# A two-layer MLP block with seven-product matrix multiplication: five row pairs instead of six first on each range of columns, and the first pair's second range computed plainly

## The chip, the cores and the metric

The kernel runs on one core of a Trainium2 chip. The metric is the device time of one execution in microseconds (us). The kernel before took 1532.34 us, the median of three runs (1531.55 to 1533.23).

The core's engines are named as the profile names them: PE is TensorE, which multiplies matrices; DVE is VectorE; ACT is ScalarE; POOL is GpSimd; SP is SyncE, whose queue issues most of the transfers (DMA).

## The reference

```python
def reference(x, w1, w2):          # x: 8 x 1024 x 1024, w1: 1024 x 4096, w2: 4096 x 1024, float32
    h = x @ w1
    h = 0.5 * h * (1 + np.tanh(np.sqrt(2 / np.pi) * (h + 0.044715 * h ** 3)))
    return (h @ w2).astype(np.float32)
```

With the batch flattened, x has 8192 rows. The first product, the gelu and the second product follow each other.

## The kernel before

**Tiling.** The 8192 rows of x are 32 *pairs* of two blocks of 128 rows (`k` is the pair, `c` the block). The 4096 columns of w1 are two halves of 2048, and each half is cut into four *ranges* of 512 (`r`, 0 to 3). A *unit* is one pair on one range: the pair's two blocks times the range's columns in both halves of w1. Both operands are cast to float16, scaled by their largest absolute value: x for each row, w1 for each range. The factors that undo this (`us`, `rs`, `up`, `rt`) go into the gelu and into the cast of its result.

**Two kinds of units.** A *plain* unit (`Plain`) has four *quarters*, one for each row block and half of w1, each of eight matmuls of 512 columns: 32 in all. It needs only the four cast blocks of w1 (B11, B21, B12, B22). All other units (`Quad1`) use Winograd's form of Strassen's method with seven products, `m1` to `m7`, of four matmuls each: 28. They also need four sums of the blocks of w1 (`sum_w1`: T1 = B12 - B11, T3 = B22 - B12, T2 = B22 - T1, T4 = B21 - T2) and four sums of the parts of x (`sum_x`), all made by VectorE. The products add up in PSUM: ScalarE copies intermediate results out (L558, L568, L577), VectorE adds others to them (L165), ScalarE applies the gelu (L483), GpSimd scales and casts the result to g (L174), and SP stores g to DRAM (L504).

**The order of units** (L669 to L677). The first pairs, `FIRST = 6` of them, run through range 0 one after another, then through range 1, 2 and 3. After that each middle pair runs through all four ranges, and the last four pairs run range by range again. Units 0 to 5 are pairs 0 to 5 on range 0, all plain; units 6 to 11 are range 1, 12 to 17 range 2, 18 to 23 range 3. The second multiplication follows when all units are done; its work on w2 is prepared during the middle units.

**An order written out by hand.** Every engine runs its instructions in the order in which they are written. `unit(u)` (L796) issues for TensorE: m1 of unit u, m7 of unit u-1, m3 of unit u-2, m2, m6 and m5 of unit u, m4 of unit u-1. Between them are seven *slots*, and `background(u, slot)` issues what `plan(u, slot, ...)` put there: preparing work for later units. So

```python
        if u < NQ:
            q.m2()
        background(u, 3)
        if u < NQ:
            q.m6()
```

means that what is planned for slot 3 of unit u stands on each engine behind the work of m2 and ahead of that of m6. Product m6 reads T2, m5 T1, m7 T3 and m4 T4. The start, up to unit 5, runs by quarters: `p` counts them, 0 to 23 (L908), the gelu of a quarter is issued right behind it, and `early(p, ...)` plans work behind quarter p. The last quarters are those of pairs 4 and 5, one pair after the other.

**Preparing a range.** For each range r from 1 on: eight pieces of w1 are loaded from GpSimd's queue (`load_w1`, L286); the largest absolute value of each is found (`look_w1`, on VectorE L151 or on ScalarE L302); VectorE takes their maximum (`widest_w1`, L312); `scale_w1` sends it through TensorE to spread it over the partitions (L158, tile `rows`) and takes the reciprocal; the pieces are cast to blocks (`cast_w1`: VectorE L176, ScalarE L172, GpSimd L174); and VectorE makes the sums T1 to T4. Range 1 is planned at L711 to L722, ranges 2 and 3 at L723 to L742 by `u = (r - 1) * FIRST - 1`. For range 2 the sums are planned in slots 4 and 6 of unit 10 and slots 1 and 3 of unit 11, for range 3 in units 16 and 17, in this order: T1, T3, T2, T4. Range 0 is made from three scales of its own for the plain units; later GpSimd brings its blocks to one scale (`even_w1`) and its sums are made (L744 to L748).

**Preparing a pair.** Blocks of the first pairs are loaded, their largest values found on ScalarE (`look_x`, L187), cast (`cast_x`) and transposed on TensorE (`turn_x_pe`, L213) in eight matmuls with a copy by ScalarE or VectorE. Pairs 4 and 5 are planned at L692 to L703. Middle pairs are transposed by DMA from SP (`turn_x`, L204) some units ahead of their first unit `a` (L750 to L762).

Of the kernel before, what the change touches and what calls it, by code (L numbers as in the profile page):

```python
# [31 lines left out]
B11, T4, B21, B22, T1, T2, T3 = range(7)  # L32
# [48 lines left out]
def kernel(  # L81
# [19 lines left out]
    NP = T // (2 * P)  # L101
    NR = I // 2 // N
    JR = N // P
    FIRST = 6
    LAST = 4
    OPEN = 4
    WARM = 52
# [569 lines left out]
    NQ = len(order)  # L677
# [11 lines left out]
    def early(p, f, *args):  # L689
        plan(p // 4, p % 4, f, *args)  # L690

    for k in range(OPEN, FIRST):  # L692
        for h in range(2):
            c = 2 * k + h
            p = (9, 12)[k - OPEN] + h
            early(p - 1, look_x, c)
            early(p, scale_x, c)
            early(p, cast_x, c, V)
            if h:
                early(p, factors_of_block, k, 0, V)  # L700
                early(p, factors_of_block, k, 1, G)
            early((2, 5)[k - OPEN], load_x, c, wpool, "w")
            early(4 * k - 2 + 2 * h - (k > 2), turn_x_pe, c, V if h else S)  # L703
    for k in first:
        for i in range(4):
            if k < 2:
                early((16, 21)[k] + i // 2, sum_x, k, (i,))
            else:
                plan(FIRST + k - 1, 2 + i, sum_x, k, (i,))

    for n in range(8):  # L711
        early((3, 4, 5, 6, 7, 8, 9, 10)[n], load_w1, 1, n)
        early((7, 8, 10, 12, 12, 13, 14, 15)[n], look_w1, 1, n, S if n in (3, 5, 7) else V)
    early(16, widest_w1, 1)
    early(17, scale_w1, 1)
    early(17, factors, 0, FIRST, 1)
    for i, n in enumerate((4, 5, 0, 1, 6, 7, 2, 3)):
        early((17, 17, 18, 18, 19, 19, 20, 21)[i], cast_w1, 1, n, S if i % 2 and n != 3 or n == 2 else V)
    early(20, sum_w1, 1, T1)
    early(22, sum_w1, 1, T2)  # L720
    plan(FIRST, 1, sum_w1, 1, T3)
    plan(FIRST, 5, sum_w1, 1, T4)  # L722
    for r in range(2, NR):  # L723
        u = (r - 1) * FIRST - 1
        for n in range(8):
            v = u - 1 + n // 2
            if r == 2:
                plan(*((4, 1), (4, 3), (5, 0), (5, 2))[n // 2], load_w1, r, n)
                look = ((5, 3), (6, 1), (6, 1), (6, 4), (6, 3), (7, 1), (7, 1), (7, 4))[n]
                plan(*look, look_w1, r, n, S if n % 2 else V)  # L730
            else:
                plan(v, 1, load_w1, r, n)
                look = (v + 2, 1) if n == 1 else (v + 1, 3 + n % 2)
                plan(*look, look_w1, r, n, S if n == 1 else V)
        plan(u + 3, 1 if r == 2 else 5, widest_w1, r)
        plan(*((u + 3, 6) if r == 2 else (u + 4, 2)), scale_w1, r)
        plan(u + 4, 2, factors, 0, FIRST, r)
        for n in range(8):
            v, slot = ((4, 3), (4, 4), (4, 5), (5, 1), (4, 3), (4, 5), (5, 3), (4, 6))[n]
            plan(u + v, slot, cast_w1, r, n, (G, S, G, S, G, V, S, V)[n])  # L740
        for i, t in enumerate((T1, T3, T2, T4)):
            plan(u + 5 + i // 2, (4, 6, 1, 3)[i], sum_w1, r, t)  # L742
# [98 lines left out]
    with tc.manual_schedule(  # L841
        engines={
            mybir.EngineType.PE, mybir.EngineType.Activation, mybir.EngineType.DVE,
            mybir.EngineType.Pool, mybir.EngineType.SP,
        }
    ):
        load_x(0, wpool, "w")
        for n in range(2):
            load_w1(0, n)
        load_x(1, wpool, "w")  # L850
        for n in range(2, 4):
            load_w1(0, n)
        V.memset(ratio, 0.0)
        V.memset(w1c, TINY)
        S.activation(out=ratio, in_=ratio, func=ACT.Gelu_apprx_tanh)
        make_identity(nc, identity)
        V.tensor_copy(out=identity16, in_=identity)
        for c in range(2, 2 * OPEN):
            load_x(c, wpool, "w")
        for n in range(4, 8):  # L860
            load_w1(0, n)
        warm_up(identity16, WARM)
        look_x(0)
        scale_x(0)
        cast_x(0, S)
        t = x16[0]
        look_w1(0, 0)
        look_w1(0, 1, V, 0)
        look_w1(0, 1, S, 1)
        turn_x_pe(0, S)  # L870
        warm_up(t, 3)
        widest_w1(0, 2)
        look_x(1)
        scale_w1(NR + 2)
        warm_up(t, 8)
        cast_w1(0, 0, V)
        cast_w1(0, 1, V)
        plain = {k: Plain(k, 0) for k in range(FIRST)}
        pa, pc = bank("pa"), bank("pc")
        plain[0].eighth(0, 0, pa)  # L880
        look_w1(0, 2, S)
        scale_x(1)
        cast_x(1, V)
        look_w1(0, 3, V, 0)
        look_w1(0, 3, S, 1)
        widest_w1(0, 3)
        look_x(2)
        warm_up(t, 3)
        turn_x_pe(1, V)
        scale_w1(NR + 3)  # L890
        plain[0].eighth(1, 0, pc)
        cast_w1(0, 2, V)
        cast_w1(0, 3, S)
        ups_of_block(0, G)
        scale_x(2)
        cast_x(2, V)
        look_x(3)
        join_halves()
        inverse_w1(slice(NR, NR + 1), G)
        plain[0].eighth(0, 1, pa)  # L900
        turn_x_pe(2, S)
        times(rs[:, 0, :, 0], xi[:, 0:2], w1j[:, NR:NR + 1], G)
        plain[0].eighth(1, 1, pc)
        scale_x(3)
        cast_x(3, V)
        look_x(4)
        look_x(5)
        quarters = [(k, 0, half, s) for s in range(2) for k in range(OPEN) for half in range(2)]  # L908
        quarters += [(k, 0, half, s) for k in range(OPEN, FIRST) for half in range(2) for s in range(2)]
        gelus = {  # L910
            0: lambda: plain[0].gelu(0, 0, plain[0].e(), pa),
            1: lambda: plain[0].gelu(1, 0, plain[0].e(), pc),
        }

        def between(p):
            if p == 2:
                scale_x(4)
                turn_x_pe(3, V)
                cast_x(4, V)
                scale_x(5)  # L920
                cast_x(5, G)
                gelus.pop(0)()
                factors_of_block(1, 0, G)
                look_x(6)
            elif p == 3:
                turn_x_pe(4, V)
                scale_x(6)
                look_w1(0, 4)
                gelus.pop(1)()
                factors_of_block(2, 0, G)  # L930
                look_x(7)
            elif p == 4:
                turn_x_pe(5, V)
                cast_x(6, V)
                scale_x(7)
                cast_x(7, G)
                look_w1(0, 5, S)
                gelus.pop(2)()
            elif p == 5:
                turn_x_pe(6, V)  # L940
                factors_of_block(3, 0, G)
                look_w1(0, 6)
                look_w1(0, 7, S)
                widest_w1(0, 1)
                gelus.pop(3)()
            elif p == 6:
                turn_x_pe(7, V)
                scale_w1(NR + 1)
                for n in range(4, 8):
                    cast_w1(0, n, S if n % 2 else V)  # L950
                inverse_w1(slice(NR + 1, NR + 2), G)
                for k in range(OPEN):
                    factors_of_block(k, 1, G)
                gelus.pop(4)()

        for p, (k, r, half, s) in enumerate(quarters):
            if p > 1:
                gelus[p] = plain[k].quarter(half, s, ("pa", "pc")[p % 2], lambda: between(p))
            if p > 6:
                for i in list(gelus)[:2]:  # L960
                    gelus.pop(i)()
            for j in (p % 4,) if p % 4 < 3 else (3, 4, 5, 6):
                background(p // 4, j)
            let_go(len(held) - 1 if len(held) > 1 and p % 2 else 0)
        now = {}
        for u in range(FIRST, NQ):
            unit(u, None)
        V.tensor_scalar(
            out=vo, in0=xm, scalar1=w2n, scalar2=SPAN, op0=ALU.mult, op1=ALU.mult
        )  # L970
        V.tensor_scalar(out=vn, in0=vo, scalar1=-1.0, scalar2=None, op0=ALU.mult)
        for u in range(NQ, NQ + 2):
            unit(u, lambda: second(3))
        let_go()
        for u in range(NQ + 2, NQ + 6):
            for slot in range(7):
                background(u, slot)
        assert not todo, todo.keys()
        second(NP * len(PRODUCTS) - done[0])
# [28 lines left out]
```

## Time and profile before

| what | value |
|---|---|
| median of three runs | 1532.34 us (1531.55 to 1533.23) |
| the profiled execution's own time | 1531.54 us |
| its span in the profile | 1529.8 us |
| TensorE busy | 1521.2 us, 99% of the span |
| VectorE busy | 1182.0 us, 77% |
| ScalarE busy | 740.3 us, 48% |
| GpSimd busy | 476.8 us, 31% |
| granted TensorE clock | 1.00 |
| units 0 to 5 end, unit 6 begins | 62.03 us |
| mean of a sum on VectorE that makes a T, 62 to 172 us (L168, 128x2048) | 1.34 us |
| mean of an add from PSUM on VectorE (L165, 128x512) | 0.68 us |
| mean of a cast of g on GpSimd, 62 to 172 us (L174, 128x512) | 0.85 us |

The profile is of one execution. A line of a time line gives the start in us, the duration in us, the engine, the line of the kernel, the operation, what it writes and reads, its shapes, how many instructions were merged, and in brackets how long the engine had been idle before it and what ended that wait. Durations overlap a little at the ends: the next instruction of an engine starts before the last one has drained, so the step from start to start is what an instruction holds its engine. On TensorE four matmuls are listed with 1.03 us, and the next product starts 0.86 us after them.

### The profile page before, as it was taken

To read this page: it belongs to the slowest core of one execution; us is meant where nothing else is said; L and a number is where in the kernel's file an instruction comes from. 1 tells how busy PE (TensorE), PEld (TensorE's weight loads), DVE (VectorE), ACT (ScalarE), POOL (GpSimd) and SP (SyncE) were. 2 spreads that over 40 slices of the span, in tenths; PEclk is the share of its full clock that TensorE was granted. 3 is DMA by queue.
4 is the path that set the end of the run, shared out by engine and by line. 5 is a ranking of instruction groups with operands and counts; after the bars stand their busy time and mean duration, and the time that the engine had idled before them with its cause. 6 is when DMAs were issued, how large, how long until landed. Compare 5 with 4: busy or idle time off the path is not lost.

```text
span 1529.8 us, 28770 instructions
## 1 busy us (share of the span) xinstructions
PE 1521.2 (99%) x10449; PEld 1018.1 (67%) x10449; DVE 1182.0 (77%) x2410; ACT 740.3 (48%) x1322; POOL 476.8 (31%) x598
## 2 busy tenths in 40 slices
PE   9999999999999999999999999999999999999999
PEld 5444444444444444444458888888888888888888
DVE  6987788777876777574348888888888888888886
ACT  8878777777777777787662111111111111111111
POOL 4689554555666656554440000000000000000000
PEclk9999999999999999999999999999999999999999
DMA  9664989877678787875995767767766866866873
GB/s 353 235 198 137 297 263 297 252 238 244 209 238 267 225 260 227 252 200 131 280 281 135 145 135 136 149 132 134 155 137 123 158 136 124 163 128 136 151 141 81
DMA packets 460992, 293.94 MB, mean 192 GB/s; under 512 B 334001, under 2 KB 429233, under 8 KB 460849
## 3 DMA queue, kind: packets, MB, share of 16 engines
q1 hardware_dynamic: 457392, 279.52, 72.2%
q0 software_dynamic: 3456, 12.58, 2.4%
q8 instruction: 81, 1.33, 0.4%
q14 instruction: 63, 0.51, 0.1%
HBM read 96.99 MB, written 114.29 MB: 138 GB/s over the span
## 4 chain that ended last, share of the span: by engine, by line
PE 97%; DVE 1%; ACT 1%; DMA 1%; SPq 0%; issue 0%; DVEq 0%; ACTq 0%
PE pa L438 52%; PE pc L438 31%; PE pb L438 14%; DMA xn<-in_x_dram 1%; ACT junk L187 0%; DVE x L176 0%; ACT e L483 0%; DVE w1c L151 0%; PE turned L213 0%; DVE up L242 0%; SPq L286 0%; ACT w L172 0%; DVE xT L220 0%; ACT xT L218 0%; SPq L183 0%
## 5 line engine op out<-in xcount | busy, mean ns | idle before, releaser
L438 PEld LDWEIGHTS <-gs 128*128 128x128 f16 x4608 | 450.8, 98 | 53.0 <-DVE gs L168 0.2
L174 POOL TENSOR_SCALAR g<-e,rs 128x512 f16<-128x512 f32 x446 | 362.8, 823 | 283.1 <-ACT e L483 258.4
L438 PEld LDWEIGHTS <-xs 128*128 128x128 f16 x1952 | 191.0, 98 | 229.7
L165 DVE TENSOR_TENSOR e<-pc,e 128x512 f32<-128x512 f32 x244 | 162.9, 686 | 202.1 <-ACT e L577 200.8
L438 PEld LDWEIGHTS <-xT 128*128 128x128 f16 x1672 | 162.8, 98 | 193.7 <-DVE xT L220 1.6
L438 PE MATMUL pa<-w,gs 128*128 128x256 f16 x2304 | 288.3, 273 | 0.0
L438 PE MATMUL pa<-w,xT 128*128 128x512 f16 (+1 forms) x1080 | 254.7, 377 | 0.5 <-ACT xT L218 0.2
L483 ACT ACTIVATE e<-e,us 128x512 f32<-128x512 f32 x366 | 251.4, 720 | 1.8 <-DVE e L165 1.8
L438 PE MATMUL pa<-w,xs 128*128 128x512 f16 x976 | 250.5, 379 | 0.0
L438 PE MATMUL pc<-w,xs 128*128 128x512 f16 x976 | 250.5, 379 | 0.0
L438 PEld LDWEIGHTS <-gT 128*128 128x128 f16 x2048 | 200.4, 98 | 23.2
L630 ACT ACTIVATE o<-pa,vo 128x256 f32<-128x256 f32 x96 | 45.3, 472 | 332.3 <-PE pa L438 332.3
L438 PE MATMUL pc<-w,gs 128*128 128x256 f16 x1536 | 193.8, 273 | 0.0
L438 PE MATMUL pa<-w,gT 128*128 128x256 f16 x1024 | 132.7, 273 | 0.0
L438 PE MATMUL pb<-w,xT 128*128 128x512 f16 x488 | 125.2, 379 | 0.0
L626 DVE SCALAR_TENSOR_TENSOR o<-pc,vo,o 128x256 f32<-128x256 f32 x160 | 77.1, 482 | 57.8 <-PE pc L438 57.8
L568 ACT COPY e<-pa 128x512 f32<-128x512 f32 x122 | 71.6, 586 | 91.3 <-PE pa L438 87.0
L168 DVE TENSOR_TENSOR gs<-gT,gs 128x1024 f16<-128x1024 f16 x160 | 109.9, 687 | 1.2 <-DMA gT<-gd 1.2
L626 DVE SCALAR_TENSOR_TENSOR o<-pa,vo,o 128x256 f32<-128x256 f32 x192 | 92.1, 481 | 19.3 <-PE pa L438 19.1
L438 PE MATMUL pb<-w,gs 128*128 128x256 f16 x768 | 99.5, 273 | 0.0
L438 PE MATMUL pc<-w,gT 128*128 128x256 f16 x768 | 99.5, 273 | 0.0
L558 ACT COPY e<-pa 128x512 f32<-128x512 f32 x122 | 70.6, 579 | 49.9 <-PE pa L438 48.2
(106 smaller groups left out, 1451.0 us busy)
## 6 DMA issues: line engine op xcount, KB each, us to landing
gd<-g SPq DMA_DIRECT2D x504, 128.0 KB, 3.3
wn<-in_w_dram SPq DMA_DIRECT2D x72, 512.0 KB, 5.2
xn<-in_x_dram SPq DMA_DIRECT2D x64, 512.0 KB, 5.5
out_dram<-o SPq DMA_DIRECT2D x62, 512.0 KB, 4.0
w<-wd SPq DMA_DIRECT2D x25, 512.0 KB, 5.8
wn<-in_w_dram POOLq DMA_DIRECT2D x24, 512.0 KB, 5.9
wd<-wt SPq DMA_DIRECT2D x24, 512.0 KB, 4.6
gT<-gd SPq DMA_TRANSPOSE x128, 6.5
```

The costliest lines, as they stand in the source:

```text
L165: V.tensor_tensor(out=o, in0=a, in1=b, op=ALU.add)
L168: V.tensor_tensor(out=o, in0=a, in1=b, op=ALU.subtract)
L174: G.tensor_scalar(out=o, in0=i, scalar1=s, scalar2=1.0, op0=ALU.mult, op1=ALU.mult)
L438: nc.tensor.matmul(bank, lhsT=left(i), rhs=right[i], start=start and i == 0, stop=i == n - 1, skip_group_check=True,)
L483: S.activation(out=e[:, c], in_=src[:, c], func=ACT.Gelu_apprx_tanh, scale=scale)
L558: S.copy(self.e11, self.pa)
L568: S.copy(self.e12, self.pa)
L626: V.scalar_tensor_tensor(out=o, in0=ps, scalar=v, in1=o, op0=ALU.mult, op1=ALU.add)
L630: S.activation(out=o, in_=ps, func=ACT.Copy, scale=v)
```

## The change

Five pairs instead of six go first through each range (`FIRST = 5`), and the first pair is plain on range 1 too, so that there are still six plain units: pairs 0 to 4 on range 0, and pair 0 on range 1. Its quarters are the last four, p = 20 to 23, and follow pair 4. Ranges 1, 2 and 3 now begin at units 5, 10 and 15, and the middle pairs at unit 20 instead of 24. Pair 5 becomes a middle pair.

With this, plans move. For pair 4 the factors of the first block of columns go to GpSimd. The sums of x of pair 0 are no longer planned at quarter 16 but in slots 2 to 5 of unit 9; those of pairs 2, 3 and 4 go one unit ahead, to units 6, 7 and 8. The looks at range 1 stand behind quarters 9 to 16, its maximum behind quarter 16, its casts behind quarters 17 to 20 in the order of the pieces, alternating VectorE and ScalarE. The maximum and the scale of range 2 are in slots 1 and 3 of unit 8 (before: slots 1 and 6 of unit 8). By `u = (r - 1) * FIRST - 1` the casts and sums of range 2 move one unit ahead (the sums to units 9 and 10) and those of range 3 two units (to units 14 and 15), and all later plans follow the first middle unit.

```diff
-    FIRST = 6
+    FIRST = 5
...
     for k in range(OPEN, FIRST):
         for h in range(2):
             c = 2 * k + h
-            p = (9, 12)[k - OPEN] + h
+            p = 9 + h
...
             if h:
-                early(p, factors_of_block, k, 0, V)
+                early(p, factors_of_block, k, 0, G)
                 early(p, factors_of_block, k, 1, G)
-            early((2, 5)[k - OPEN], load_x, c, wpool, "w")
+            early(2, load_x, c, wpool, "w")
...
     for k in first:
         for i in range(4):
-            if k < 2:
-                early((16, 21)[k] + i // 2, sum_x, k, (i,))
+            if k == 1:
+                early(21 + i // 2, sum_x, k, (i,))
             else:
-                plan(FIRST + k - 1, 2 + i, sum_x, k, (i,))
+                plan(FIRST - 1 + (k or FIRST), 2 + i, sum_x, k, (i,))
 
     for n in range(8):
-        early((3, 4, 5, 6, 7, 8, 9, 10)[n], load_w1, 1, n)
-        early((7, 8, 10, 12, 12, 13, 14, 15)[n], look_w1, 1, n, S if n in (3, 5, 7) else V)
+        early((3, 4, 4, 5, 6, 7, 8, 9)[n], load_w1, 1, n)
+        early(9 + n, look_w1, 1, n, S if n in (3, 5, 7) else V)
     early(16, widest_w1, 1)
     early(17, scale_w1, 1)
     early(17, factors, 0, FIRST, 1)
-    for i, n in enumerate((4, 5, 0, 1, 6, 7, 2, 3)):
-        early((17, 17, 18, 18, 19, 19, 20, 21)[i], cast_w1, 1, n, S if i % 2 and n != 3 or n == 2 else V)
-    early(20, sum_w1, 1, T1)
+    for n in range(8):
+        early(17 + n // 2, cast_w1, 1, n, S if n % 2 else V)
+    early(21, sum_w1, 1, T1)
     early(22, sum_w1, 1, T2)
-    plan(FIRST, 1, sum_w1, 1, T3)
-    plan(FIRST, 5, sum_w1, 1, T4)
+    plan(FIRST + 1, 1, sum_w1, 1, T3)
+    plan(FIRST + 1, 5, sum_w1, 1, T4)
...
-        plan(u + 3, 1 if r == 2 else 5, widest_w1, r)
-        plan(*((u + 3, 6) if r == 2 else (u + 4, 2)), scale_w1, r)
-        plan(u + 4, 2, factors, 0, FIRST, r)
+        plan(*((u + 4, 1) if r == 2 else (u + 3, 5)), widest_w1, r)
+        plan(u + 4, 3 if r == 2 else 2, scale_w1, r)
+        plan(u + 4, 3 if r == 2 else 2, factors, 0, FIRST, r)
...
-        plain = {k: Plain(k, 0) for k in range(FIRST)}
+        plain = {(k, 0): Plain(k, 0) for k in range(FIRST)}
+        plain[0, 1] = Plain(0, 1)
...
         quarters += [(k, 0, half, s) for k in range(OPEN, FIRST) for half in range(2) for s in range(2)]
+        quarters += [(0, 1, half, s) for half in range(2) for s in range(2)]
...
-                gelus[p] = plain[k].quarter(half, s, ("pa", "pc")[p % 2], lambda: between(p))
+                gelus[p] = plain[k, r].quarter(half, s, ("pa", "pc")[p % 2], lambda: between(p))
...
-        for u in range(FIRST, NQ):
+        for u in range(FIRST + 1, NQ):
             unit(u, None)
```

## The prediction

> **What bounds the kernel now.** The page first: TensorE is busy for 1521.2 of 1529.8 us.
>
> ```profile
> span 1529.8 us, 28770 instructions
> PE 1521.2 (99%) x10449; PEld 1018.1 (67%) x10449; DVE 1182.0 (77%) x2410; ACT 740.3 (48%) x1322; POOL 476.8 (31%) x598
> PE 97%; DVE 1%; ACT 1%; DMA 1%; SPq 0%; issue 0%; DVEq 0%; ACTq 0%
> ```
>
> So nothing can be won but gaps in TensorE's stream, and lost by new ones. Both kernels do six plain units and 122 of seven products, so the matmuls stay. The time line of TensorE is the second view: I look for gaps behind quarter 16, where the change begins (45.45 us), and for the pace.
>
> ```profile
> 45.45 1.89 PE L438 MATMUL pa<-w,xT 128*128 128x512 f16 x8
> 48.91 0.61 PE L213 MATMUL turned<-identity,x 128*128 128x128 f16 x8
> 51.09 0.29 PE L158 MATMUL rows<-identity,w1a 128*128 128x128 f32 x1 [1.57 <-DVE w1a L312]
> 51.22 1.89 PE L438 MATMUL pa<-w,xT 128*128 128x512 f16 x8
> 54.67 0.61 PE L213 MATMUL turned<-identity,x 128*128 128x128 f16 x8
> 55.12 1.89 PE L438 MATMUL pa<-w,xT 128*128 128x512 f16 x8
> 62.03 1.03 PE L438 MATMUL pa<-w,xT 128*128 128x512 f16 x4
> 92.35 1.03 PE L438 MATMUL pa<-w,xs 128*128 128x512 f16 x4
> 128.72 1.03 PE L438 MATMUL pa<-w,xs 128*128 128x512 f16 x4
> ```
>
> A quarter takes 1.726 us (51.22 to 52.95), a matmul 0.216, a product of four 0.863, a unit 6.04. After the 1.57 us gap the stream has none: all that VectorE and ScalarE do is hidden. The last two lines are product m6 of units 11 and 17. For these I read when T2 is ready in those units, in the time lines of VectorE and ScalarE:
>
> ```profile
> 92.81 0.68 DVE L165 TENSOR_TENSOR e<-pc,e 128x512 f32<-128x512 f32 x1
> 93.41 1.21 DVE L168 TENSOR_TENSOR w<-w 128x2048 f16<-128x2048 f16 x1
> ...
> 127.87 0.69 DVE L165 TENSOR_TENSOR e<-pc,e 128x512 f32<-128x512 f32 x1 [1.32 <-ACT e L577]
> 128.48 1.22 DVE L168 TENSOR_TENSOR w<-w 128x2048 f16<-128x2048 f16 x1
> ```
>
> ```profile
> 48.92 0.82 ACT L483 ACTIVATE e<-pa,up 128x256 f32<-128x256 f32 x2
> 57.84 1.15 ACT L172 ACTIVATE w<-wn,w1i 128x1024 f16<-128x1024 f32 x1
> 60.56 0.84 ACT L483 ACTIVATE e<-pa,up 128x256 f32<-128x256 f32 x2 [1.00 <-PE pa L438]
> 127.25 0.59 ACT L577 COPY e<-pa 128x512 f32<-128x512 f32 x1
> ```
>
> The two w sums (93.41, 128.48) are T2 of ranges 2 and 3. They end at 94.62 and 129.70, which is 2.27 and 0.98 us *after* m6 of the unit in which they are made. It costs nothing now, because the range starts a unit later (12, 18). With five pairs the ranges start at units 10 and 15, and T2 stays in slot 1 of these very units. That is my main reason.
>
> **The change part by part.** Times of one execution (1531.54 us, span 1529.8; the median of the three runs is 0.80 above it).
>
> *Pair 5 leaves the start.* Its 16 transposes on TensorE go: 48.91 and 54.67 are each followed 0.44 to 0.45 us later by what could run, so -0.9. Its two loads leave SP's queue at 23 us, its two looks (1.05 each) ScalarE, its casts and factors VectorE. They return in units 12 to 19, with two loads and two transposes by DMA in SP's queue, ahead of stores of g. The later transpose is issued at the end of unit 16 and first read in slot 5 of unit 18, over 10 us later; the 52 of this kind took 4.8 in the median and 9.5 at most to land, so nothing. Uncovered, a load that is late by its median of 5.5 would cost as much.
>
> *The maximum of range 1 first.* Now it waits behind a copy and two sums of x on VectorE. In the changed order the last look (piece 7, ScalarE) stands behind the gelu of quarter 16. That quarter ends at 47.34; a gelu starts 0.10 later (60.56 against 60.46) and holds ScalarE 0.71; look 1.06 and its read-out end at 49.30; maximum 0.15 and the step to TensorE 0.15: rows at 49.63 instead of 51.09. That is -1.46, 0.45 of it the transposes counted above. So -1.0, and with them -1.9. Ends: -1.57 if the wait goes, 0 if piece 7, whose transfer landed at 47.86, comes late. Factors of pair 4 on GpSimd: three of 0.26, behind all eight issues of range 1's loads and ahead of casts of g that wait for ScalarE: nothing; uncovered 0.8.
>
> *Pair 0 plain on range 1.* Quarter 20 (now at 49.63 + 0.13 + 2 x 1.726 = 53.21) needs the blocks themselves. VectorE's four casts follow the scale (50.4) by 0.5 and take 0.66 to 0.95 each: done by 54.7, ahead of use. ScalarE's four alternate with gelus: piece 7 stands behind the gelu of quarter 20, so relative to the start of quarter 21 it begins at 0.26 (0.16 tail, 0.10 step) + 0.57 = 0.83 and ends at 1.98; its matmul is the seventh, at 6 x 0.216 = 1.30. A stall of 0.7. Piece 5 by the same sum has 0.18 to spare. Ends 0.3 (an overlap of gelu and cast) and 1.2 (piece 5 late as well). Range 1's T sums then have some 3 us before unit 6 wants them.
>
> *Range 2's scale moves from the end of unit 8 into it.* The maximum follows the add at +2.60 to +3.20 (79.41 in unit 9, which began at 76.81), then 0.15 and 0.15: rows at +3.5, wanted at +3.45. 0.1; ends 0 and 0.5 (unit 8 of before had the maximum end at +3.84).
>
> *T2 of range 2.* From the first add behind VectorE's casts to the end of T2 took 8.02 us (86.60 to 94.62). The changed order puts one look of range 3 (1.13) into that chain: 9.15. It began 3.75 into unit 10, for the two casts beside GpSimd's took 2.2. Now the scale is half a unit sooner and the adds can't start before +2.6; by the work listed ahead (two adds, four sums of x, six small ones, two casts) they start between +2.6 and +3.6 of unit 9. I take 3.0: T2 at 12.15, 6.1 into unit 10, m6 wanted at 3.45: a stall of 2.6. Ends: 0.95 (T2 right behind the add: 2.60 + 0.60 + 1.21 - 3.45) and 4.2 (start at 3.6, one T sum at 2.14, the slowest of the 16 between 50 and 180 us).
>
> *T2 of range 3.* 0.98 as it stands, plus the look at x of pair 5, which the change puts on ScalarE right ahead of the two copies that the add waits for; ScalarE had no idle time there (124.96 to 127.73). A look holds it 1.05. Stall 2.0; ends 0.95 and 3.0. Range 0's sums, for the middle pairs, end a unit before use: nothing; with a backlog of 6 us they would cost the excess.
>
> Sum: -1.9 + 0.7 + 0.1 + 2.6 + 2.0 = +3.5 on the profiled time, 1535.0, and 1535.8 on the median (+0.23%). A measurement tells about 0.2% (3.1 us) from no change.
>
> A row that speaks against the change: sums of x at 0.41 us stand beside others at 0.8 and 1.25, T sums at 1.21 beside 2.14, wherever GpSimd is busy. The Trainium skill (SBUF — State Buffer, "SBUF: two separate sides") says that a VectorE operation with two SBUF inputs or in a two-port mode and a GpSimd operation exclude each other for a whole instruction. The trace agrees: 2.14 is 1.21 plus 0.93, and a GpSimd cast of g takes 0.69 to 1.3. If it hit every sum, the result would be the third rival's.
>
> **The rivals.**
> *Floor.* VectorE and ScalarE arrive in units 10 and 15 with no backlog, so each T2 follows the add at once: 0.95 each. -1.9 + 0.8 + 1.9 = +0.8, 1533.1, no change. It decides when the add of m7 starts by 2.7 us into the unit both times. For it: range 3's VectorE idled 1.32 before that add. Against: in range 2 T2 was 2.27 late, with one operation less ahead of it.
> *All hidden.* The T sums are finished ahead in spite of their place, and only piece 7's cast stalls: -1.9 + 0.7 = -1.2, 1531.1. Against: T2 stands behind an add that needs m7 of the same unit. Only if the early gain were also larger than worked out could it be over 0.2% faster: the gap and the transposes together are 2.5 us.
> *Port.* GpSimd meets the casts and all three T sums of range 2 (3 x 0.93) and one in range 3: +3.7 more, +7.2, 1539.5. For it: GpSimd now has range 3's issues and casts in the same units, and its scaling of range 0 (1.1 to 2.1 each) right behind range 3's casts.
>
> **How the numbers follow.** Forecast 0.50 (its own range 1534.6 to 1537.6; a fifth of it under +3.1), floor 0.22, hidden 0.05, port or other backlog 0.23. Slower: 0.40 + 0.23 = 0.63. Same: 0.10 + 0.22 + 0.03 = 0.35. Faster 0.02. Range: half of the floor's cases and the dearest tenth left out, 1533.0 to 1538.8.
>
> **What would show it.** TensorE: rows at about 49.6, a gap of about 0.7 in the quarter of w pieces 4 to 7 (55 to 57 us), unit 6 near 60.8; then gaps ahead of a pa<-w,xs product near 85 and 118 us, ended by VectorE's L168 w, of 2.6 and 2.0 us; no others. If the second pair is under 1.0 each, the floor was right; if a gap is ended by something else (a load, a copy, L165), I missed a queue; if ScalarE's L577 is not late in unit 15, the look did not matter.

## The result and the profile after

| | before | after |
|---|---|---|
| median | 1531.69 us (6 runs, 1531.03 to 1533.23) | 1543.70 us (6 runs, 1541.45 to 1544.32) |
| ratio to before, 95% interval | | 1.0076 (1.0066 to 1.0087) |
| profiled execution | 1531.54 us, span 1529.8 | 1541.45 us, span 1539.7 |

The change costs 12.0 us in the medians and 9.9 us between the two profiled executions. The forecast was 1535.8 (+3.5), with a range up to 1538.8. The profiled execution of after is the fastest of its six.

The page of after: TensorE is busy for 0.8 us more than before (1522.0 against 1521.2 us), while the span grows by 9.9, so most of the new time is idle time. Matmuls at a lower clock count as busy.

```profile
span 1539.7 us, 28746 instructions
PE 1522.0 (99%) x10433; PEld 1016.9 (66%) x10433; DVE 1179.2 (77%) x2408; ACT 738.1 (48%) x1319; POOL 473.5 (31%) x599
```

The waits of after, of which these lines hold all of TensorE's from quarter 16 on (columns: who waited <- what ended the wait: us in total, times, longest; two of the three waits at `rows` lie ahead of quarter 16):

```profile
PE pa L438 <- DVE w L168: 8.2, 2, 6.0
PE rows L158 <- DVE w1a L312: 1.8, 3, 0.9
PE pc L438 <- ACT w L172: 0.6, 1, 0.6
```

The first line is new and holds nearly everything: two waits for a sum of w on VectorE, one of 6.0 us. The time line of TensorE in after shows where they stand:

```profile
46.15 1.89 PE L438 MATMUL pa<-w,xT 128*128 128x512 f16 x8
50.36 0.29 PE L158 MATMUL rows<-identity,w1a 128*128 128x128 f32 x1 [0.59 <-DVE w1a L312]
57.69 0.59 PE L438 MATMUL pc<-w,xT 128*128 128x512 f16 x2 [0.57 <-ACT w L172]
61.57 1.03 PE L438 MATMUL pa<-w,xT 128*128 128x512 f16 x4
85.03 1.03 PE L438 MATMUL pb<-w,xT 128*128 128x512 f16 x4
92.07 1.89 PE L438 MATMUL pa<-w,xs 128*128 128x512 f16 x4 [6.01 <-DVE w L168]
93.75 1.63 PE L438 MATMUL pc<-w,xs 128*128 128x512 f16 x4
95.21 1.89 PE L438 MATMUL pa<-w,xT 128*128 128x512 f16 x8
122.95 1.03 PE L438 MATMUL pb<-w,xT 128*128 128x512 f16 x4
126.16 1.04 PE L438 MATMUL pa<-w,xs 128*128 128x512 f16 x4 [2.18 <-DVE w L168]
```

From quarter 16 (46.15) to `rows` it is now 4.21 us (before 5.64). Unit 6 begins at 61.57. Product m2 of unit 10 starts at 85.03 and m6 could follow at 85.89, but it waits for T2 until 92.07: 6.18 lost. Then m6 takes 1.68 us (92.07 to 93.75) and m5 1.46, where a product takes 0.863: another 1.41. In unit 15, m6 comes at 126.16 instead of 123.81: 2.35 lost. Behind that nothing new is listed.

Why do m6 and m5 take so long? In stretches of 5 us (start and end, length; busy us and instructions of PE, PEld, DVE, ACT, POOL; granted clock; share of the DMA engines; GB/s) after shows:

```profile
85.00:90.00 5.00, 1.06 (x5) 0.29 (x3) 5.00 (x7) 3.47 (x7) 4.96 (x5) 0.81 0.81 279
90.00:95.00 5.00, 2.93 (x8) 1.04 (x9) 5.00 (x7) 0.95 (x2) 2.18 (x3) 0.51 0.66 209
95.00:100.00 5.00, 5.00 (x25) 2.29 (x24) 2.92 (x5) 3.23 (x6) 2.03 (x4) 1.00 0.28 102
```

Behind the wait of 6.01 us the granted clock is 0.51, and it is back at 1.00 in the stretch from 95 us on. The wait is paid for a second time, in slow matmuls.

And why is T2 so late? The time line of VectorE in after, from the factors of range 2 in unit 8 to T2:

```profile
76.09 2.79 DVE L242 TENSOR_SCALAR rs<-xi,w1j 128x10 f32<-128x10 f32 x1
79.11 0.91 DVE L168 TENSOR_TENSOR xs<-xT,xs 128x512 f16<-128x512 f16 x1
79.94 3.37 DVE L176 TENSOR_SCALAR w<-wn,w1i 128x1024 f16<-128x1024 f32 x2
83.24 1.27 DVE L165 TENSOR_TENSOR e<-pc,e 128x512 f32<-128x512 f32 x2
...
90.80 1.21 DVE L168 TENSOR_TENSOR w<-w 128x2048 f16<-128x2048 f16 x1
```

The time line of GpSimd in after over the same time:

```profile
76.55 2.21 POOL L174 TENSOR_SCALAR w<-wn,w1i 128x1024 f16<-128x1024 f32 x2
78.74 1.84 POOL L174 TENSOR_SCALAR g<-e,rs 128x512 f16<-128x512 f32 x2
80.56 1.11 POOL L174 TENSOR_SCALAR w<-wn,w1i 128x1024 f16<-128x1024 f32 x1
81.65 2.21 POOL L174 TENSOR_SCALAR g<-e,rs 128x512 f16<-128x512 f32 x2
```

A multiplication of ten numbers for each partition, 0.23 and 0.25 us in ranges 1 and 3, takes 2.79 and ends (78.88) with GpSimd's two casts of w (78.76). The next sum of x takes 0.91 where others take 0.41, and two casts take 3.37 (2.28 before), all while GpSimd casts without a pause. So the adds at the head of the chain start at 83.24, 6.85 us into unit 9 (which began at 76.39), and not 3.0. From there to the end of T2 (92.01) it is 8.77 us; I had said 9.15. The chain has the length forecast and starts 3.85 late.

In range 3 ScalarE's look at x stands where it was expected. First ScalarE's time line, then VectorE's, of after:

```profile
121.75 1.05 ACT L187 ACTIVATE junk<-xn 128x1024 bf16<-128x1024 f32 x1
```

```profile
123.89 0.69 DVE L165 TENSOR_TENSOR e<-pc,e 128x512 f32<-128x512 f32 x1 [2.27 <-ACT e L577]
124.50 1.60 DVE L168 TENSOR_TENSOR w<-w 128x2048 f16<-128x2048 f16 x1
```

VectorE has nothing to do for 2.27 us until ScalarE's copies come, and then makes T2 in 1.60 instead of 1.21.

The account between the two profiled executions, in us: start up to quarter 16 +0.70; quarter 16 to unit 6 -1.16 (piece 7's stall of 0.73 in it); unit 10 +6.18 and +1.41; unit 15 +2.35; together 9.5 of 9.9. The first 0.70 lies ahead of the change's first effect, in waits of the opening microseconds that vary between executions: in after and in kernels 7 and 9 below, which issue the same up to there, `rows` comes at 50.4, 49.8 and 51.3.

### The profile page after: what moved, and what is told of

The parts are those of the page before. It is cut to its first block, busy times and chain, and to the rows that moved or that the text cites. A ratio compares the mean times of both kernels' runs of the same rounds, so it can differ in the third digit from the quotient of the medians.

```text
span 1539.7 us, 28746 instructions
## 1 busy us (share of the span) xinstructions
PE 1522.0 (99%) x10433; PEld 1016.9 (66%) x10433; DVE 1179.2 (77%) x2408; ACT 738.1 (48%) x1319; POOL 473.5 (31%) x599
## 4 chain that ended last, share of the span: by engine, by line
PE 97%; DVE 1%; ACT 1%; DMA 1%; issue 0%; SPq 0%; ACTq 0%
PE pa L438 52%; PE pc L438 31%; PE pb L438 14%; DMA xn<-in_x_dram 1%; DVE w L168 0%; DVE e L165 0%; ACT w L172 0%; PE turned L213 0%; ACT e L483 0%; DVE rs L242 0%; SPq L286 0%; ACT junk L187 0%; DVE xs L168 0%; DVE w L176 0%; ACT junk L302 0%
```

## Experiments

All ratios are to the kernel before, measured beside each kernel on the same chip (1531.41 us in the first four experiments, 1531.48 in the next four, 1531.46 in the last two). Theory A: the loss is T2 standing in the first unit of its range, made dear by VectorE's late start beside GpSimd, and by the clock behind the gap. Its rivals: another place is the cause (pair 0 plain, pair 5, the start), or the late start has another reason (the look, the sums of x).

**1. T2 ahead of T3.** After, with T2 in the slot of T3:

```diff
-        for i, t in enumerate((T1, T3, T2, T4)):
+        for i, t in enumerate((T1, T2, T3, T4)):
```

> The changed kernel with one order altered: in ranges 2 and 3 VectorE makes T1, T2, T3, T4 in place of T1, T3, T2, T4, so that T2 stands in slot 6 of the unit ahead of the range instead of slot 1 of its first unit. If the place of T2 is the cause of both gaps and VectorE's backlog sets the size of the first: in unit 15 T2 ends near 121.6 us, ahead of m6, and the gap of 2.2 us goes; in unit 10 T2 ends 1.8 us earlier (a sum and an add less ahead of it) and the gap of 6.0 us becomes about 4.2, with less or no time at half clock. Together 4 to 6 us below the changed kernel. If something else holds m6, both gaps stay and the time is the changed kernel's.

Measured: 1536.91 us (1536.84 to 1537.66), 1.0039 (1.0024 to 1.0054). The wait in unit 15 is gone, that in unit 10 is 4.27, as TensorE's time line of this kernel shows:

```profile
89.57 1.89 PE L438 MATMUL pa<-w,xs 128*128 128x512 f16 x4 [4.27 <-DVE w L168]
```

By the medians the place of T2 is worth 6 to 7 us of the 12. The traces show 4.1 of it as shorter waits (m6 4.44 late in unit 10 in place of 6.18, not late in unit 15); no trace shows the rest, which differs between executions. What is left of the wait in unit 10 does not hang on the order of the sums, since T2 already follows T1, from which it is made. One expectation was missed: the shorter wait brought more time at the low clock and not less. Behind m6 (89.57) and m5 (91.25) of this kernel stand two products,

```profile
92.96 2.71 PE L438 MATMUL pa<-w,xT 128*128 128x512 f16 x8
```

and the next one comes at 95.50. These four lose 2.48 us in all, where m6 and m5 of after lost 1.41.

**2. The wait filled.** After, with 48 matmuls of no use issued into the wait, which only keep TensorE busy:

```diff
+    plan(2 * FIRST, 3, lambda: warm_up(w1set[1, B11][:, 0, :], 48))
```

> The changed kernel with 48 matmuls of 256 columns on data that nobody reads, behind m2 of unit 10, so that TensorE works for about 5.2 us of the 6 us for which it waits for T2. If the wait also lowers the clock and the half clock costs extra time behind it: the granted clock stays at 1.00, m6 and m5 of unit 10 take 0.86 us each in place of 1.68 and 1.46, and the time falls by 1.4 us or more (more where other executions stay longer at half clock), with less spread. If the clock adds nothing: the same time.

Measured: 1540.51 us (1539.57 to 1541.26), 1.0060 (1.0043 to 1.0077). All its executions lie below the fastest of after's; its excess over before is 9.1 us, 2.9 less than after's. T2 is as late as ever (m6 at 91.47), but in the stretches of this kernel the clock stays at 1.00, and falls at the unfilled wait of 2.18 us in unit 15 instead:

```profile
85.00:90.00 5.00, 5.00 (x46) 4.29 (x44) 5.00 (x7) 2.88 (x6) 5.00 (x4) 1.00 0.77 282
90.00:95.00 5.00, 4.24 (x24) 2.04 (x22) 5.00 (x7) 1.81 (x3) 2.60 (x5) 1.00 0.71 233
120.00:125.00 5.00, 2.82 (x13) 1.10 (x11) 3.11 (x4) 3.06 (x6) 5.00 (x6) 0.93 0.16 52
125.00:130.00 5.00, 5.00 (x19) 1.94 (x17) 2.83 (x5) 3.30 (x6) 5.00 (x5) 0.72 0.31 84
```

In unit 10 m6 and m5 are back at 0.88 and 0.86 us. So the slow matmuls behind the wait follow from the idle time. That work of no use is cheaper than idling there is shown by the medians alone: the traced execution saves 1.41 us in unit 10 and loses 1.70 behind the wait in unit 15, and lies 0.3 below that of after.

**3. The factors out of the way.** After, with range 2's factors one unit later:

```diff
-        plan(u + 4, 3 if r == 2 else 2, factors, 0, FIRST, r)
+        plan(*((u + 5, 6) if r == 2 else (u + 4, 2)), factors, 0, FIRST, r)
```

> The changed kernel with range 2's two factor operations on VectorE moved from slot 3 of unit 8 to slot 6 of unit 9, away from the first two casts of range 2 on GpSimd; the second of them took 2.79 us there, 0.25 elsewhere. If GpSimd's casts hold up whatever VectorE has in their way: the sums of x or VectorE's own casts of w now take the delay, the chain to T2 starts 0 to 1.5 us sooner and the gap in unit 10 stays above 4.5 us. If it is this small operation alone that suffers: the casts end 2.5 us sooner, the gap falls to about 3.5 us and the time by 2.5 us or more.

Measured: 1543.14 us (1540.41 to 1544.04), 1.0076 (1.0061 to 1.0091). Next to nothing is won, and the time lines of VectorE and of GpSimd in this kernel say why:

```profile
76.06 3.14 DVE L176 TENSOR_SCALAR w<-wn,w1i 128x1024 f16<-128x1024 f32 x2
84.53 3.10 DVE L168 TENSOR_TENSOR xs<-xT,xs 128x512 f16<-128x512 f16 x1
```

```profile
84.67 2.69 POOL L174 TENSOR_SCALAR g<-e,rs 128x512 f16<-128x512 f32 x4
```

The casts now meet GpSimd's, and take 3.14. The adds do start at 79.12 instead of 83.24, but a sum of x further down the chain takes 3.10 instead of 0.41, from the start to the end of four casts of g. The wait is still 5.33. So the loss does not belong to the factors: other operations that stand beside GpSimd's casts can take it over.

**4. T2 in its own unit, in the kernel before.** The one place in question alone, with six pairs first: range 2's sums one unit later.

```diff
-            plan(u + 5 + i // 2, (4, 6, 1, 3)[i], sum_w1, r, t)
+            plan(u + 5 + i // 2 + (r == 2), (4, 6, 1, 3)[i], sum_w1, r, t)
```

> The kernel before with one plan altered: range 2's four sums one unit later (T2 in slot 1 of unit 12, the first unit of range 2 there), six pairs and all else as before. If the place of T2 alone makes the gap, a gap appears ahead of m6 of unit 12; VectorE has no casts and no scale in units 11 and 12, so it should be near its floor, 0.95 to 1.5 us, and the time 1 to 1.5 us above before. If the backlog were the same everywhere, it would be 2.5 us or more; if the place does not matter, none.

Measured: 1532.57 us (1530.95 to 1533.77), 1.0008 (0.9999 to 1.0018). TensorE's time line of this kernel in unit 12:

```profile
100.10 1.04 PE L438 MATMUL pa<-w,xs 128*128 128x512 f16 x4 [0.89 <-DVE w L168]
```

That is the 0.95 of the *floor*: with no backlog on VectorE, T2 in its own unit costs about 1 us (m6 comes 1.06 late), and the granted clock stays at 1.00.

**5. No casts of w on GpSimd.** After, with the three pieces that GpSimd casts for range 2 cast by ScalarE:

```diff
-            plan(u + v, slot, cast_w1, r, n, (G, S, G, S, G, V, S, V)[n])
+            plan(u + v, slot, cast_w1, r, n, (S if r == 2 else G, S, S if r == 2 else G, S, S if r == 2 else G, V, S, V)[n])
```

> The changed kernel with range 2's three casts of w on GpSimd given to ScalarE, in the same slots. If GpSimd's casts are what holds VectorE in unit 8: the factor operation that took 2.79 us takes about 0.25, VectorE's two casts about 0.7 to 1.1 each in place of 1.65, the adds of unit 9 start 3 to 4 us sooner, and the gap in unit 10 is set by ScalarE, which has three casts of 1.04 more in two units: 1 to 4 us in place of 6. If VectorE is late by its own amount of work: these operations keep their durations and the gap stays near 6 us.

Measured: 1541.08 us (1540.98 to 1542.52), 1.0066 (1.0051 to 1.0081). VectorE's time line of this kernel:

```profile
75.83 0.42 DVE L242 TENSOR_SCALAR rs<-xi,w1j 128x10 f32<-128x10 f32 x1
...
76.64 1.41 DVE L176 TENSOR_SCALAR w<-wn,w1i 128x1024 f16<-128x1024 f32 x2
82.58 1.29 DVE L165 TENSOR_TENSOR e<-pc,e 128x512 f32<-128x512 f32 x2 [4.54 <-ACT e L577]
```

This shows the cause of the late start: without GpSimd's casts of w the factors take 0.42 instead of 2.79 and two casts 1.41 instead of 3.37, and VectorE is done at 78.05. But then it waits 4.54 for ScalarE, which has the casts now, and TensorE's time line of this kernel has the bill:

```profile
78.34 1.02 PE L438 MATMUL pa<-w,xs 128*128 128x512 f16 x4 [1.17 <-ACT e L568]
82.12 1.02 PE L438 MATMUL pa<-w,xs 128*128 128x512 f16 x4 [1.03 <-ACT e L558]
86.35 1.02 PE L438 MATMUL pa<-w,xs 128*128 128x512 f16 x4 [0.61 <-ACT e L568]
91.41 1.89 PE L438 MATMUL pa<-w,xs 128*128 128x512 f16 x4 [2.31 <-DVE w L168]
```

The casts can't be had for nothing on ScalarE either in these two units.

**6. The look out of the chain.** After, with range 3's look at piece 0, which stands between the adds and T2, a unit later:

```diff
-                look = (v + 2, 1) if n == 1 else (v + 1, 3 + n % 2)
+                look = (v + 2, 1) if n == 1 else (v + 2, 3) if n == 0 else (v + 1, 3 + n % 2)
```

> The changed kernel with one look of VectorE (first piece of range 3) moved from slot 3 of unit 9 behind T2, to slot 3 of unit 10. If VectorE's queue is what T2 waits for, each operation taken out of it is worth its own length: the gap in unit 10 falls by about 1.1 us to 4.9, and the time by 1.1 to 1.5. If GpSimd's casts of g push back (each VectorE operation moved meets one of them), the gap falls by less than 0.5.

Measured: 1540.51 us (1540.18 to 1544.55), 1.0066 (1.0049 to 1.0083); the wait is 5.45. That lies between the two expectations. Of the look's 1.13 us in the chain, half comes off the wait (0.56): two sums of x behind it took 0.90 and 0.91 instead of 0.42 and 0.82 beside GpSimd. The median lies lower by more than the wait does, and the highest execution above all of after's. The clock goes with this: three executions had a mean clock of 0.999 and took 1540.2 to 1540.5 us, the fourth 0.996 and 1544.6.

**7. All four kinds of late work moved.** The edits of 1 and 6, and pair 0's sums of x in unit 7 instead of 9, and piece 7 of range 1 cast by VectorE:

```diff
-                plan(FIRST - 1 + (k or FIRST), 2 + i, sum_x, k, (i,))
+                plan(FIRST - 1 + (k or 3), 2 + i, sum_x, k, (i,))
-        early(17 + n // 2, cast_w1, 1, n, S if n % 2 else V)
+        early(17 + n // 2, cast_w1, 1, n, S if n % 2 and n < 7 else V)
```

> The changed kernel with four plans altered: T1, T2, T3, T4 in this order in ranges 2 and 3, the look of the last entry later, pair 0's sums of x in unit 7 in place of unit 9, and piece 7 of range 1 cast by VectorE. If place and queue explain all gaps: no gap behind quarter 20, none in unit 15, and in unit 10 T2 follows T1 with two casts, three adds and nothing else ahead: 83.2 + 1.9 + 2 x 1.13 in the changed kernel's times, a gap of about 2 us, because GpSimd still holds VectorE in unit 8. The time is then about 1 us below to 2 us above the kernel before. If gaps have other causes, more remains.

Measured: 1531.20 us (1530.94 to 1533.51), 1.0000 (0.9991 to 1.0010). The wait of some 2 us that I still expected in unit 10 did not come. From quarter 16 on TensorE waits only for the maxima in front of `rows`, 0.59, 0.39 and 0.17 us, of which the time line shows the two of ranges 2 and 3:

```profile
72.93 0.32 PE L158 MATMUL rows<-identity,w1a 128*128 128x128 f32 x1 [0.39 <-DVE w1a L312]
102.78 0.32 PE L158 MATMUL rows<-identity,w1a 128*128 128x128 f32 x1 [0.17 <-DVE w1a L312]
```

GpSimd still slows VectorE in this kernel (two casts take 2.62), but the same factors lose far less beside the same two casts of w. First VectorE's time line, then GpSimd's:

```profile
75.37 1.03 DVE L242 TENSOR_SCALAR rs<-xi,w1j 128x10 f32<-128x10 f32 x1
```

```profile
75.24 2.71 POOL L174 TENSOR_SCALAR w<-wn,w1i 128x1024 f16<-128x1024 f32 x2 [0.29 <-DVE w1i L317]
```

With that, with pair 0's four sums gone and with T2 ahead of T3, the chain has room for it: T2 is ready ahead of m6. The edits for pair 0's sums and for piece 7 were not measured alone. So five pairs and a second plain unit for pair 0 cost nothing as such; the whole +12 is where four pieces of preparing work were put. With them placed better the kernel equals the one before, no more.

**8. The look at x in unit 15.** After, with the look at pair 5's first block in slot 1 of unit 15 instead of slot 5 of unit 14:

```diff
-            plan(a - 6 + late + h, 5, look_x, c)
+            plan(*((a - 5, 1) if c == 10 else (a - 6 + late + h, 5)), look_x, c)
```

> The changed kernel with the look at the first block of pair 5 moved on ScalarE behind the two copies that unit 15's add waits for (slot 1 of unit 15). If that look is what makes the gap in unit 15 larger than the 0.98 us read from the profile of before: the gap falls from 2.2 to about 1.1 us and the time by about 1.1, or more if the shorter gap no longer lowers the clock. If not, the gap stays at 2.2.

Measured: 1541.23 us (1541.02 to 1542.25), 1.0066 (1.0049 to 1.0083). In TensorE's time line the wait in unit 15 is halved, that in unit 10 stays:

```profile
91.53 1.89 PE L438 MATMUL pa<-w,xs 128*128 128x512 f16 x4 [6.03 <-DVE w L168]
125.93 1.04 PE L438 MATMUL pa<-w,xs 128*128 128x512 f16 x4 [1.09 <-DVE w L168]
```

2.18 is 1.09 for the place of T2 and 1.09 for the look, which is the sum of the prediction (0.98 + 1.05) within 0.15. The excess over before falls from 12.0 to 9.8 us, by twice the wait that was saved; the surplus is not explained. In unit 10 the wait is as long as in after, but the low clock costs 2.82 us behind it in place of 1.41, since it reaches into the two products behind m5, whose successor comes at 97.80:

```profile
94.92 3.05 PE L438 MATMUL pa<-w,xT 128*128 128x512 f16 x8
```

**9. The scales half a product later.** Kernel 7, with the scales of ranges 2 and 3 and what follows them one slot later:

```diff
-        plan(u + 4, 3 if r == 2 else 2, scale_w1, r)
-        plan(u + 4, 3 if r == 2 else 2, factors, 0, FIRST, r)
+        plan(u + 4, 4 if r == 2 else 3, scale_w1, r)
+        plan(u + 4, 4 if r == 2 else 3, factors, 0, FIRST, r)
...
+            slot = 4 if r == 2 and slot == 3 and v == 4 else slot
```

> The last kernel (T sums in another order, less ahead of them) with the scales of ranges 2 and 3 one slot later, so that TensorE does not wait for the maximum in unit 8 (0.39 us of idle time there) and unit 13 (0.17). If these waits are all that is left of the new gaps: TensorE waits only behind quarter 17 (0.6 us), T2 still comes in time, and the time is 0.5 to 0.8 us below that kernel, 0.8 to 1.5 below the kernel before. If the half slot makes the casts of range 2 late, a new gap appears in unit 10 and the time is above before.

Measured: 1531.58 us (1530.34 to 1534.53), 1.0000 (0.9991 to 1.0009). The two waits of 0.39 and 0.17 are gone from the profile, and the time does not show the 0.5 to 0.8 us expected: the start differs by more between executions (`rows` of range 1 at 51.33 here, at 49.77 in kernel 7's). A part is given back besides: T2 ends at 86.38, and m6 of unit 10 comes 0.29 late.

**10. Only the maximum first, in the kernel before.**

```diff
-                early((16, 21)[k] + i // 2, sum_x, k, (i,))
+                early((18, 21)[k] + i // 2, sum_x, k, (i,))
```

> The kernel before with one part of the change alone: range 1's maximum ahead of the sums of x of pair 0, which go two quarters later (behind quarters 18 and 19). If the 1.57 us gap behind quarter 17 was VectorE's queue, it falls to 0.5 to 0.7 (a copy of turned x still stands ahead) and the time by 0.9 to 1.1 us. If ScalarE's last look holds the maximum, the gap stays above 1.2 us.

Measured: 1530.29 us (1529.93 to 1531.01), 0.9994 (0.9985 to 1.0003). TensorE's time line of this kernel has no wait in front of `rows`, where the kernel before has 1.57:

```profile
49.83 0.61 PE L213 MATMUL turned<-identity,x 128*128 128x128 f16 x8
50.52 0.29 PE L158 MATMUL rows<-identity,w1a 128*128 128x128 f32 x1
50.65 1.89 PE L438 MATMUL pa<-w,xT 128*128 128x512 f16 x8
```

The step beyond the transposes' own 0.44 falls from 1.74 to 0.25, 1.5 us; the median falls by 1.2. It is the lowest median of all kernels here, but its interval still holds no change.

## Why the prediction was wrong, and which of its steps held

*Pair 5's transposes and the maximum first*, -1.9: right. `rows` came 1.43 us sooner after quarter 16 (forecast 1.46), 0.59 of the wait staying; kernel 10, which keeps the transposes, shows 1.5 for the order alone, as no wait is left there. (The terms given for `rows` add up to 49.60 and not 49.63; nothing hangs on it.)

*Pair 0 plain on range 1*, 0.7: right, 0.73 at the piece named, ended by ScalarE's cast. Kernel 7 removes the stall with that one cast moved.

*Range 2's scale*, 0.1: right in unit 8 (0.01).

*T2 of range 3*, 2.0: right, 2.35 with the 0.39 by which T2 itself took longer; kernel 8 splits it as the sum did.

*T2 of range 2*, 2.6: this step failed, with 6.18 measured. Place, releaser and chain length were as forecast (8.77 against 9.15), but the sum took the chain's start as "between +2.6 and +3.6 of unit 9", and it was +6.85. I listed the work ahead with its free durations, plus the 2.2 to 2.3 us that two casts took in the kernel before. The small operations were counted as small. Kernel 5 shows what was missing: with no casts of w on GpSimd, the factors and casts take 1.83 instead of 6.16. In after, the excess is 2.54 for the factors, 0.50 for a sum of x and 1.09 for the two casts over their 2.28, together 4.1, for a chain that starts 3.85 late. The scale had been moved half a unit to where GpSimd's own casts follow it at once, so both engines start their casts of the same range together, with GpSimd's casts of g between them. The rows for it were in the profile of before (two casts 2.28, a sum of x 1.25 instead of 0.41), but I took the largest excess for one operation as one GpSimd instruction, 0.93. It can be more: two in after (2.79 - 0.25 = 2.54, beside casts of 2.21 together) and four in kernel 3 (3.10 - 0.41 = 2.69). It need not be: in kernel 7 the same factors lost 0.78 beside the same two casts, and in after VectorE went on behind the second of seven casts that GpSimd made without a pause. What decides how many it is stays open.

The Trainium skill (SBUF — State Buffer, "SBUF: two separate sides") says that the operation that comes second on the port shared by GpSimd and VectorE is blocked for the other's whole instruction. The runs agree that the two hold each other up, and differ in the length: VectorE's operation sat through two and through four of GpSimd's instructions. That the port is what they dispute is the page's account; the runs show only that GpSimd's casts are the cause.

*A term that was absent*: the clock. I priced every gap at its own length. A wait of 6 us left the clock at about half for m6 and m5, 1.41 us in the profiled execution. Kernel 2 against after puts it near 2.9 in the medians, though kernel 2 loses time at its own low clock in unit 15; kernel 8, traced with the same wait, lost 2.82. This may also be most of what the profiled execution lies below the median: its mean clock was 0.997, that of four of the other five 0.996. How long the clock stayed low in those is not on record, since only one execution was traced.

*The rivals.* Port had the right mechanism at other places: it priced three T sums of range 2 at 0.93 more each, and these took their free 1.21 in after; the factors, a sum of x and the casts were hit in their stead. Floor is what the kernel before gives with the same place of T2 (0.89 in kernel 4): the condition I named, no backlog, decided it. Nothing was hidden.

That the change could not win much was right: its gain is the wait at `rows` and the transposes, 1.9 us without piece 7's stall. The trace of kernel 7 shows it whole (quarter 16 to unit 6 takes 14.70 us instead of 16.58), and the two later waits at `rows` give 0.98 of it back. What is left is too little for the medians: kernels 7 and 9 cannot be told from before.

## What to carry to other kernels

Work of two engines that hold each other up must not be summed from free durations: where one has several instructions in a row, put more than one of them into the dear end of the range as the possible delay of any single operation beside it, even of a tiny one. When a matrix stream with no slack gets a new wait, price the matmuls behind it at the lower clock too: waits of 2.18 to 6.03 us cost from nothing to 2.8 us more here. And when a shift of whole plans by one unit costs more than it should, look for the items that come late: here four edits of a line each, two of them also measured alone, gave back all 12 us.

## What was not expected of the hardware

A wait for GpSimd is not limited to one of its instructions: an operation on VectorE of 0.25 us took 2.79, one of 0.41 took 3.10, each ending about when two or four of GpSimd's casts did. The factors began 0.46 us before the first of the two casts is listed, while GpSimd was still issuing transfers (75.03 to 76.51); whether these held them too was not tested. The two engines also swap the loss: while VectorE's chain ran (85 to 91 us in after), four casts of g took 5.42 us, where four took 2.69 while VectorE was held up in kernel 3.

The length of idle time at which the clock falls is not sharp. A wait of 2.18 us left it at 1.00 in after and brought 0.93 and then 0.72 in kernel 2, with the start of m5 1.53 us behind that of m6:

```profile
124.15 1.74 PE L438 MATMUL pa<-w,xs 128*128 128x512 f16 x4 [2.18 <-DVE w L168]
```

The wait of 1.57 us in the kernel before left no mark, and 2.31 us behind three shorter waits in kernel 5 gave a stretch of 0.66. Nor does the loss follow the length of the wait: 1.70 us behind 2.18 in kernel 2, 2.48 behind 4.27 in kernel 1, 1.41 behind 6.01 in after, 2.82 behind 6.03 in kernel 8. The Trainium skill (TensorE: Matmul & The Clock Gate, "What's actually happening") gives the windows in which activity is watched as about 3.4 us long and free-running, and the low clock as the state behind at least one idle window. That a fall comes after 2.18 us in one execution and not in another goes with windows that start at no fixed point; that it comes after 2.18 us at all does not go with a window of 3.4 us that has to be idle, and there the measurement decides. No run here shows the windows themselves.
